# Attention and retention on 64 rows: the products of two heads issued alternately

## The chip, the cores and the metric

The kernel runs on one core of a Trainium2 chip. The metric is the device time of one execution, in microseconds; of several runs the median is given. One further execution was recorded by the hardware profiler; its span is the time from its first to its last instruction. The engines are named as in the profile: PE is the tensor engine (PEld its loading of the stationary operand), DVE the vector engine, ACT the scalar engine, POOL the third compute engine, SP the one that issues transfers.

## The reference, cut to what matters

The kernel computes one inference step of a two-layer diffusion backbone on 256 latent and 128 context tokens with 1024 features, in float32. Layer 0 projects the normed tokens to two groups of eight heads of 64 features each. Group A is attention, group B retention, a linear attention with a decay by distance:

```
s_loc = einsum('bhrjqd,bhrwjkd->bhrjqwk', qg, band(k)) * scale + bias     # latent queries: a window of latents
s_ctx = einsum('bhrjqd,bhpd->bhrjqp', qg, k_ctx) * scale                  # ... and all context keys
p = softmax(concatenate([s_loc, s_ctx]))                                  # context queries: context keys alone
o_A = p @ v

att = einsum('bhid,bhjd->bhij', q, k) * dmask                             # group B, per direction
o_B = att @ v + (q * q_dec) @ s                                           # s: the cached state
o_B = rmsnorm(o_forward + o_backward) * silu(g)
y = concatenate([o_A, o_B]) @ w_out
```

Each sub-layer stands between two RMS norms and is followed by a SwiGLU channel mixer; layer 1 is a gated linear recurrence. Both are as before in the change.

## The kernel before, in words

Activations lie feature-major: 128 features of a tile in the partitions, 384 tokens along them. A tile of queries or keys thus holds two heads: the even one in partitions 0 to 63, the odd one in 64 to 127. Products with weights are split into three (`wh*hh`, `wh*hl`, `wl*hh`) in float32r; the products of attention and retention are plain float32, and each shows as two records in the trace.

The program is written as streams (generators) that yield instructions. A list scheduler (`Machine`, lines 102 to 199) merges them into one order per engine: it keeps a rough clock of each engine and takes next the stream whose head could start first; `margin` says how long before its turn a product's operands must be ready. A tuple that a stream yields is emitted in one piece. `products()` (line 1428) is the stream of the weight products: the in-projection in parts (`va` and `vb` token-major, with the tokens stationary, then the rest), gates, output projection. Weights are split into a high and a low part by ACT (`wh`, line 237) and DVE or, while a norm is under way, POOL (`wl`, lines 245 and 243). In free places DVE forms the modulation of later sub-layers by dot products (`mod_dve`, line 604, tile `mscr`), PE forms another part of it (`mod_pe`, tile `mraw`).

- `attention(h)`, line 952, one stream per head: three products into two of the eight PSUM banks (latent queries 0 to 127 with the 384 keys, the context queries with the context keys, latent queries 128 to 255), then bias, maximum, exponential and scaling on DVE and ACT, and seven transposes (`cb,as`, line 223). There are two score buffers `as`, so two heads can be under way. `attended(hp)`, line 1000, multiplies the values of two heads; its outputs have 64 rows, and the two heads are issued alternately already (`pt,va`, `pt,vc`).
- `retention(hp)`, line 1018, one stream per pair of heads, two sets of buffers. Lines 1055 to 1074 take the heads one after the other: decay matrix on DVE and ACT, two products of 256 columns into one bank (line 1066), their multiplication by the decay (`ro`, `at`), a product of 128 columns into another bank (line 1071), its multiplication (`kd`). The products with the values close the pair.
- `retention_norm`, line 1085: sums of squares of all heads on PE, root on ACT, reciprocal on DVE, spread back by PE (`scr,cse`), then per tile two multiplications and the split into `hh` and `hl`, for which the output projection waits.

The next norm and the channel mixer's first products follow (`Norm`, `ffn_products`).

Of the kernel before, what the change touches and what calls it, by code (L numbers as in the profile page):

```python
"""Two-layer hybrid diffusion backbone (neighbourhood attention + retention, then HGRN2) on one core.

Activations are kept feature-major: [128 features of a tile, tile, 384 tokens], the 256 latent
tokens first and the 128 context tokens after them. Products with the weights run as float32r:
each operand is split exactly into a high and a low part (w = wh + wl, x = xh + xl) and
wh*xh + wh*xl + wl*xh is accumulated.

The program is written as streams of instructions (generators). A list scheduler merges them into
one order per engine: it keeps a rough clock per engine and per region of memory, and of the next
instructions of all streams it takes the one that could start first. Tile adds the waits.  # L10

Each sub-layer starts its first group of products on x * g * (1 + scale), before the norm of x is
known; the reciprocal norm multiplies those products when they leave PSUM, and the shift comes in
as two more columns of the moving operand (one per condition). Later products use the normed h.
"""
# [18 lines left out]
P = 128  # L34
D = 1024
KT = 8            # feature tiles of D
NS = 256          # latent tokens
NP = 128          # context tokens
NT = NS + NP
NX = NT + 2       # and a column for the shift of either condition  # L40
FT = 22           # feature tiles of D_FF
# [6 lines left out]
# ------------------------------------------------------------------ the list scheduler  # L48
def region(ap):
    """name of the memory, first and last partition, first and last element"""  # L50
# [12 lines left out]
class Op:  # L63
    """one instruction: engine, call, what it writes and reads, time it holds the engine"""
# [8 lines left out]
# the order of emission: when loads may start, how long before its turn a stream's product must be ready  # L73
# [15 lines left out]
# from the end of an instruction to the start of one that waits for it, by engine: leaving, arriving  # L89
LEAVE = {"PE": 0.2, "DVE": 0.13, "ACT": 0.14, "POOL": 0.08, "SP": 0.9}  # L90
ARRIVE = {"PE": 0.15, "DVE": 0.0, "ACT": 0.0, "POOL": 0.05, "SP": 0.0}
# the tensor engine runs at half its clock at first
# [9 lines left out]
class Machine:  # L102
# [53 lines left out]
    def advance(self, s):  # L156
        """make the next instructions of a stream known; False if it waits, None if it is over"""
# [51 lines left out]
class Build:  # L209
    """instructions, not yet emitted"""  # L210
# [4 lines left out]
    def mm(self, out, lhsT, rhs, start=True, stop=True):  # L215
        n = width(rhs)
        cost = n * (1 if rhs.dtype == F32R and n >= 256 else 4) / 2400
        cost *= {32: 0.3, 64: 0.56}.get(out.shape[0], 1.0)
# [69 lines left out]
# ------------------------------------------------------------------ plans of weight chunks  # L288
def plan_kouter(ms, nk, n=4):
    """groups of n output tiles, k outside"""  # L290
    flat = [(k, m) for g in range(0, len(ms), n) for k in range(nk) for m in ms[g:g + n]]
    return [flat[i:i + 8] for i in range(0, len(flat), 8)]


def plan_kinner(ms, nk):
    """one output tile after the other"""
# [4 lines left out]
# even in-projection: 28 tiles: qa 0-3 ka 4-7 va 8-11 qb 12-15 kb 16-19 vb 20-23 gb 24-27  # L301
PLAN_E1 = plan_kouter([4, 5, 6, 7, 0, 1], KT, 6)
PLAN_E2 = plan_kouter([8, 9, 10, 11], KT)          # va, token-major
PLAN_E3 = plan_kinner([2, 3], KT)
PLAN_E4 = plan_kinner([12, 16, 13, 17, 14, 18, 15, 19], KT)
PLAN_E5 = plan_kouter([20, 21, 22, 23], KT)        # vb, token-major
PLAN_E6 = plan_kinner([24, 25, 26, 27], KT)
PLAN_EVEN = [PLAN_E1, PLAN_E2, PLAN_E5, PLAN_E3, PLAN_E4, PLAN_E6]
# odd in-projection: 40 tiles: q 0-7 ff 8-15 fb 16-23 i 24-31 g 32-39
PLAN_O1 = plan_kouter([0, 8, 16, 1, 9, 17], KT, 6)  # L310
PLAN_O2 = [plan_kouter(list(range(24 + 4 * g, 28 + 4 * g)), KT) for g in range(2)]      # i, token-major
# [159 lines left out]
def emit_all(nc, tc, ctx, io, outs):  # L471
# [480 lines left out]
    def attention(h):  # L952
# [42 lines left out]
        if h % 2 == 1:  # L995
            M.spawn(attended(hp), 3, margin=M_ATT)
# [596 lines left out]
```

## Time and profile before

| | us |
|---|---|
| runs, median of 3 (lowest, highest) | 1171.53 (1168.97, 1172.67) |
| span of the profiled execution | 1170.4 |
| PE busy | 1102.9 |
| DVE busy | 862.5 |
| ACT busy | 535.5 |
| POOL busy | 211.9 |

The profile gives no other time of its execution than the span, which lies inside the range of the runs. "Busy" is the union of an engine's instructions; matmuls are pipelined and the ends of their records are modelled, so the distance from the start of one product to the start of the next says more than a record's length. All float32 products of attention and retention have the line of the helper that records them, L219; they are told apart by the tiles: `bank<-ka,qa` are attention's scores, `bank<-qk` retention's.

### The profile page before, as it was taken

Reading aid. Unit: us, or ns where it says so; the run is one execution under the profiler, and the core shown is the slowest. Engines: PE = TensorE matmul, PEld = TensorE weight load, DVE = VectorE, ACT = ScalarE, POOL = GpSimd, SP = SyncE. Lnnn points to the kernel's source line nnn. Section 1 sums busy time; section 2 is a strip of 40 time slices with the busy share of each in tenths; the row PEclk is TensorE's granted clock in tenths of the full one; section 3 lists DMA queues with packets and bytes.
Section 4 is the critical chain, followed back from the end, with each engine's and each line's share of the span. In section 5 each row is a group of like instructions: output and inputs, shape, how many; then the busy total and the mean of one; then the engine's idle time right before and its main releaser. Section 6 shows DMA issues by size and latency. Waiting matters only on the chain. (4 is left out here: it accounts for less than half of the span.)

```text
span 1170.4 us, 18358 instructions
## 1 busy us (share of the span) xinstructions
PE 1102.9 (94%) x7012; PEld 1018.2 (87%) x7012; DVE 862.5 (74%) x1615; ACT 535.5 (46%) x1010; POOL 211.9 (18%) x192
## 2 busy tenths in 40 slices
PE   7999999998799999999959999999997999999996
PEld 5768887887799999998947988889987999999995
DVE  2698887678999999884898589997778644443343
ACT  3675544445433333334654555665555433333231
POOL 1210000036200000000655134352027200000001
PEclk9999999989899999999989999999999999999998
DMA  8965545343377677674231332222222343334331
GB/s 338 367 210 204 178 159 179 119 163 115 122 259 241 238 237 247 228 264 171 99 99 55 104 100 83 86 82 95 96 91 90 110 131 119 129 123 135 129 115 54
DMA packets 49688, 180.43 MB, mean 154 GB/s; under 512 B 6561, under 2 KB 13729, under 8 KB 43073
## 3 DMA queue, kind: packets, MB, share of 16 engines
q1 hardware_dynamic: 49536, 179.18, 44.9%
q8 instruction: 55, 0.90, 0.3%
q14 instruction: 33, 0.26, 0.1%
q0 software_dynamic: 64, 0.08, 0.0%
HBM read 174.79 MB, written 3.41 MB: 152 GB/s over the span
## 5 line engine op out<-in xcount | busy, mean ns | idle before, releaser
L219 PE MATMUL bank<-hh,wh 128*128 128x384 f32 (+1 forms) x1248 | 441.0, 353 | 11.4 <-DVE wb L262 8.5
L219 PE MATMUL bank<-hl,wh 128*128 128x384 f32 (+1 forms) x1248 | 427.6, 343 | 6.0 <-DVE hl L245 6.0
L219 PE MATMUL bank<-hh,wl 128*128 128x384 f32 (+1 forms) x1248 | 426.0, 341 | 0.7 <-POOL wl L243 0.7
L245 DVE TENSOR_TENSOR wl<-wr,wh 128x1024 fp32r<-128x1024 f32 x190 | 233.8, 1231 | 121.9 <-ACT wh L237 121.9
L237 ACT ACTIVATE wh<-wr 128x1024 fp32r<-128x1024 f32 x216 | 227.7, 1054 | 157.1 <-PE bank L219 116.2
L219 PEld LDWEIGHTS bank<-hh,wh 128*128 128x128 f32 x1248 | 238.8, 191 | 26.9 <-DVE wb L262 9.1
L219 PEld LDWEIGHTS bank<-hl,wh 128*128 128x128 f32 x1248 | 239.3, 192 | 8.5 <-DVE hl L245 8.1
L219 PEld LDWEIGHTS bank<-hh,wl 128*128 128x128 f32 x1248 | 239.7, 192 | 1.1 <-POOL wl L243 1.1
L258 DVE SCALAR_TENSOR_TENSOR mscr<-mraw,msb 128x1024 f32<-128x1024 f32 x128 | 157.9, 1233 | 2.3 <-ACT msb L237 1.2
L243 POOL TENSOR_TENSOR wl<-wr,wh 128x1024 fp32r<-128x1024 f32 x26 | 64.3, 2476 | 513.0 <-ACT wh L237 507.6
L219 PE MATMUL bank<-gh,wl 128*128 128x384 f32 x352 | 117.6, 334 | 0.0
L219 PE MATMUL bank<-gl,wh 128*128 128x384 f32 x352 | 117.6, 334 | 0.0
L219 PE MATMUL bank<-gh,wh 128*128 128x384 f32 x352 | 117.6, 334 | 0.0
L219 PEld LDWEIGHTS bank<-gh,wh 128*128 128x128 f32 x352 | 66.1, 188 | 0.0
L219 PEld LDWEIGHTS bank<-gl,wh 128*128 128x128 f32 x352 | 66.1, 188 | 0.0
L219 PEld LDWEIGHTS bank<-gh,wl 128*128 128x128 f32 x352 | 66.1, 188 | 0.0
L237 ACT ACTIVATE fs<-bank 128x384 f32<-128x384 f32 x38 | 18.7, 492 | 89.1 <-PE bank L219 89.1
L237 ACT ACTIVATE gh<-fs 128x384 fp32r<-128x384 f32 x44 | 22.9, 519 | 72.3 <-DVE fs L245 58.3
L237 ACT ACTIVATE scr<-bank 128x384 f32<-128x384 f32 x44 | 21.7, 492 | 61.6 <-PE bank L219 60.8
L219 PE MATMUL bank<-wh,hl 128*128 128x512 f32 x96 | 40.4, 421 | 9.2 <-DVE hl L245 9.1
L243 POOL TENSOR_TENSOR x<-x,fy 128x384 f32<-128x384 f32 x4 | 4.5, 1150 | 242.6 <-DVE fy L245 242.6
L245 DVE TENSOR_TENSOR fs<-bank,fs 128x384 f32<-128x384 f32 x38 | 21.2, 558 | 36.2 <-PE bank L219 35.0
(222 smaller groups left out, 1432.8 us busy)
## 6 DMA issues: line engine op xcount, KB each, us to landing
mraw<-in_w_mod SPq DMA_DIRECT2D x48, 1024.0 KB, 5.9
wr<-in_w_ffn_in SPq DMA_DIRECT2D x88, 512.0 KB, 3.3
wr<-in_w_ffn_out SPq DMA_DIRECT2D x44, 512.0 KB, 3.4
wr<-in_w_in_odd SPq DMA_DIRECT2D x40, 512.0 KB, 3.3
wr<-in_w_in_even SPq DMA_DIRECT2D x28, 512.0 KB, 5.3
wr<-in_w_out_even SPq DMA_DIRECT2D x8, 512.0 KB, 3.3
wr<-in_w_out_odd SPq DMA_DIRECT2D x8, 512.0 KB, 3.3
bias<-in_bias SPq DMA_DIRECT2D x8, 384.0 KB, 4.0
```

Source lines behind the costliest of these rows:

```text
L219: return Op("PE", lambda: self.nc.tensor.matmul(out, lhsT=lhsT, rhs=rhs, start=start, stop=stop), [out], [lhsT, rhs], cost + 0.004)
L237: return Op("ACT", lambda: self.nc.scalar.activation(out, in_, func, **kw), outs, ins, 0.1 + width(in_) / 1200, table)
L243: return Op("POOL", lambda: self.nc.gpsimd.tensor_tensor(out=out, in0=a, in1=b, op=op), [out], [a, b], 0.12 + n * 0.0021)
L245: return Op("DVE", lambda: self.nc.vector.tensor_tensor(out=out, in0=a, in1=b, op=op), [out], [a, b], 0.06 + n / 960)
L258: return Op("DVE", lambda: self.nc.vector.scalar_tensor_tensor(out=out, in0=a, scalar=s, in1=b, op0=op0, op1=op1, **kw), outs, ins, 0.1 + ...
```

## The change

Attention's stream is per pair of heads: it takes two score buffers and four banks and issues the three products of both heads alternately, the even head from partitions 0 to 63, the odd one from 64 to 127, into different banks; what follows per head is a stream of its own, `probabilities`. Retention takes two decay buffers and two banks, forms both decay matrices first, issues its products alternately, and puts the 128-column products into the same two banks as the 256-column ones. The scheduler's cost of a product with 64 rows is set as that of one with 64 columns. Comments are removed throughout.

```diff
-        cost *= {32: 0.3, 64: 0.56}.get(out.shape[0], 1.0)
+        cost *= {32: 0.3, 64: 0.56}.get(min(out.shape[0], lhsT.shape[0]), 1.0)
...
-    def attention(h):
-        hp, j = h // 2, h % 2
-        a, b = 64 * j, 64 * j + 64
+    def attention(hp):
         qa, ka = L0.qa, L0.ka
-        res, = yield from L0.heads.take()
+        yield lambda: "ctx" in ev and ("qa", hp) in ev and ("ka", hp) in ev
+        res = yield from L0.heads.take(2)
+        bs = yield from banks.take(4)
+        for out, q, k in ((lambda j: bs[2 * j][:, :NT], (0, P), (0, NT)), (lambda j: bs[2 * j + 1][:, :NT], (P, NS), (0, NT)),
+                          (lambda j: bs[2 * j][:, NT:512], (NS, NT), (NT, 512))):
+            yield tuple(I.mm(out(j), qa[64 * j:64 * j + 64, hp, q[0]:q[1]], ka[64 * j:64 * j + 64, hp, k[0]:k[1]]) for j in range(2))
+        for j in range(2):
+            M.spawn(probabilities(2 * hp + j, res[j], bs[2 * j], bs[2 * j + 1]), P_ATT + 0.01 * (2 * hp + j), margin=M_ATT)
+    def probabilities(h, res, b0, b1):
         s, mx, sm = res
-        yield lambda: "ctx" in ev and ("qa", hp) in ev and ("ka", hp) in ev and len(L0.biases) > 0
-        bias = L0.biases.popleft()
-        b0, b1 = yield from banks.take(2)
-        yield (I.mm(b0[:, :NT], qa[a:b, hp, 0:P], ka[a:b, hp, :NT]),)
-        yield (I.mm(b0[:, NT:512], qa[a:b, hp, NS:NT], ka[a:b, hp, NT:512]),)
-        yield (I.mm(b1[:, :NT], qa[a:b, hp, P:NS], ka[a:b, hp, :NT]),)
+        yield lambda: len(L0.biases) > 0 and L0.biases[0][0] == h
+        bias = L0.biases.popleft()[1]
...
-        for j in range(2):
+        rows = [slice(64 * j, 64 * j + 64) for j in range(2)]
+        dts = yield from scr.take(2)
+        for j, dt in enumerate(dts):
             h = 2 * hp + j
-            a, e = 64 * j, 64 * j + 64
-            dt, = yield from scr.take()
             yield I.ts(dt, cse[:, E_DP:E_DP + NT], L0.rdb[:, 0, h:h + 1], MUL)
...
-            b, = yield from banks.take()
-            for n, s_ in ((0, 1), (1, 0)):
-                yield I.mm(b[:, NS * n:NS * n + NS], k[a:e, P * s_:P * s_ + P], q[a:e, :NS])
+        bs = yield from banks.take(2)
+        yield tuple(I.mm(bs[j][:, NS * n:NS * n + NS], k[rows[j], P * s_:P * s_ + P], q[rows[j], :NS])
+                    for n, s_ in ((0, 1), (1, 0)) for j in range(2))
+        for j in range(2):
             for n in range(2):
-                yield I.tt(ats[j][:, n], b[:, NS * n:NS * n + NS], dt[:, P * n:P * n + NS], MUL)
-            banks.give(b)
-            b, = yield from banks.take()
-            yield I.mm(b[:, :P], k[a:e, NS:NT], q[a:e, NS:NT])
-            yield I.tt(ap_[:, j], b[:, :P], dt[:, P:2 * P], MUL)
-            banks.give(b)
-            scr.give(dt)
+                yield I.tt(ats[j][:, n], bs[j][:, NS * n:NS * n + NS], dts[j][:, P * n:P * n + NS], MUL)
+        yield tuple(I.mm(bs[j][:, :P], k[rows[j], NS:NT], q[rows[j], NS:NT]) for j in range(2))
+        for j in range(2):
+            yield I.tt(ap_[:, j], bs[j][:, :P], dts[j][:, P:2 * P], MUL)
+        banks.give(*bs)
+        scr.give(*dts)
...
-        for h in range(8):
-            M.spawn(attention(h), P_ATT + 0.01 * h, margin=M_ATT)
+        for hp in range(4):
+            M.spawn(attention(hp), P_ATT + 0.02 * hp, margin=M_ATT)
```

The scheduler makes a new order of it, from the first attention products to the middle of layer 1. On PE, the end of a value group (`pt`) and the scores of one head that follow it stood so before:

```order
L219 MATMUL bank_63<-pt_147,vc 64x256
L219 MATMUL bank_63<-pt_146,va 64x128
L219 MATMUL bank_63<-pt_147,va 64x128
L219 MATMUL bank_68<-ka,qa 128x384
L219 MATMUL bank_68<-ka,qa 128x128
L219 MATMUL bank_66<-ka,qa 128x384
L219 MATMUL bank_70<-wh_108,hh 128x512
```

and so now, for the second pair:

```order
L219 MATMUL bank_67<-pt_147,vc 64x256
L219 MATMUL bank_67<-pt_146,va 64x128
L219 MATMUL bank_67<-pt_147,va 64x128
L219 MATMUL bank_65<-ka,qa 128x384
L219 MATMUL bank_66<-ka,qa 128x384
L219 MATMUL bank_69<-ka,qa 128x128
L219 MATMUL bank_64<-ka,qa 128x128
L219 MATMUL bank_68<-wh_109,hh 128x512
```

These are the last four products of the pair; its first two, into banks 69 and 64, stand ahead of the value group. The third and the fourth pair stand in the same way, the first pair in one piece. Behind the second pair's last products 15 token-major and 24 feature-major weight products follow before its first transposes.

In retention on PE, a head's two groups before:

```order
L219 MATMUL bank_70<-qk 128x256 x2
L219 MATMUL bank_65<-hh,wh_108 128x384
L219 MATMUL bank_65<-hl,wh_108 128x384
L219 MATMUL bank_65<-hh,wl_111 128x384
L219 MATMUL bank_69<-qk 128x128
```

and a pair's now:

```order
L219 MATMUL bank_64<-qk 128x256
L219 MATMUL bank_63<-qk 128x256
L219 MATMUL bank_64<-qk 128x256
L219 MATMUL bank_63<-qk 128x256
L219 MATMUL bank_67<-hh,wh_110 128x384
L219 MATMUL bank_67<-hl,wh_110 128x384
L219 MATMUL bank_67<-hh,wl_113 128x384
L219 MATMUL bank_65<-qd_156,s_153 128x256 x2
L219 MATMUL bank_64<-qk 128x128
L219 MATMUL bank_63<-qk 128x128
```

Four products now stand between two weight products where two stood, and the 128-column ones return to the banks of the others. Between a pair's two groups the order has 6, 6, 3 and 12 weight products.

On DVE, from the last retention step (`kd`) to the operand of the retention norm's product (`scr<-rs,cb`), before:

```order
L245 TENSOR_TENSOR kd_154<-bank_65,scr_92 128x128
L245 TENSOR_TENSOR wl_111<-wr_105,wh_108 128x1024
L268 RECIPROCAL rs_86<-rs_86 128x96
L245 TENSOR_TENSOR scr_91<-rs_86,cb 128x384
L245 TENSOR_TENSOR wl_112<-wr_106,wh_109 128x1024
```

and now:

```order
L245 TENSOR_TENSOR kd_154<-bank_67,scr_88 128x128
L245 TENSOR_TENSOR mod_80<-macc_131,bmod 128x2x2
L258 SCALAR_TENSOR_TENSOR mod_80<-mod_80,gn 128x2
L258 SCALAR_TENSOR_TENSOR mscr_130,macc_132<-mraw_103,msb_129 128x1024 x3
L245 TENSOR_TENSOR wl_111<-wr_105,wh_108 128x1024
L268 RECIPROCAL rs_86<-rs_86 128x96
L258 SCALAR_TENSOR_TENSOR mscr_130,macc_132<-mraw_103,msb_129 128x1024
L245 TENSOR_TENSOR wl_112<-wr_106,wh_109 128x1024
L245 TENSOR_TENSOR scr_91<-rs_86,cb 128x384
```

Four dot products of the first phase moved here from earlier places, and a weight split passed the norm's operand. Further on, at the start of the channel mixer, the second pair of modulation chunks that PE forms (`mraw`) moved behind the first 15 weight products, and 54 weight products instead of 87 stand on PE ahead of the second norm's last step. In layer 1 the order of the mixers' products differs in places; the counts of all instructions on PE, ACT and SP are the same, and two weight splits moved from POOL to DVE.

## Rows read from the trace of the kernel before

**Rows 1.** From the page: busy time, share of the span and instructions of each engine.

```profile
PE 1102.9 (94%) x7012; PEld 1018.2 (87%) x7012; DVE 862.5 (74%) x1615; ACT 535.5 (46%) x1010; POOL 211.9 (18%) x192
```

**Rows 2.** Busy time by stretch: from and to (us from the span's start), length, busy time of PE, PEld, DVE, ACT and POOL (instructions), granted clock of PE, share and GB/s of DMA.

```profile
74.60:130.00 55.40, 55.08 (x300) 42.97 (x298) 51.27 (x108) 34.66 (x72) 0.00 (x0) 1.00 0.64 210
130.00:195.00 65.00, 65.00 (x393) 54.00 (x393) 54.99 (x116) 28.75 (x55) 0.00 (x0) 1.00 0.50 165
195.00:212.00 17.00, 17.00 (x106) 13.99 (x105) 9.96 (x19) 10.72 (x16) 0.00 (x0) 1.00 0.38 147
...
226.00:249.40 23.40, 22.10 (x165) 20.21 (x163) 16.94 (x32) 9.60 (x17) 2.36 (x1) 1.00 0.50 164
249.40:256.30 6.90, 6.47 (x19) 6.07 (x20) 6.90 (x18) 4.34 (x15) 2.98 (x3) 0.51 0.50 209
```

**Rows 3.** PE's longest wait from 67 to 226 us: total, times, longest.

```profile
PE bank L219 <- ACT qa L237: 1.1, 1, 1.1
```

**Rows 4.** The modulation's dot products on DVE (instructions that write mscr) in the stretches 74.6 to 130, 130 to 195 and 195 to 212 us: sum of their lengths, sum and mean of DVE's busy time.

```profile
sum 137.40, DVE 39.31; mean DVE 13.10
```

**Rows 5.** PE in order of time around a head that stands alone (`ka,qa`), its first transposes (`cb,as`), and a value group (`pt`) with the next head behind it: start, us, operation, shapes, count of records.

```profile
82.39 0.39 PE L219 MATMUL bank<-wl,hh 128*128 128x512 f32 x1
82.63 0.39 PE L219 MATMUL bank<-wh,hl 128*128 128x512 f32 x1
82.94 1.78 PE L219 MATMUL bank<-ka,qa 64*128 64x384 f32 x6
84.65 0.50 PE L219 MATMUL bank<-wh,hh 128*128 128x512 f32 x1
84.99 0.39 PE L219 MATMUL bank<-wl,hh 128*128 128x512 f32 x1
...
87.55 0.60 PE L223 MATMUL bank<-cb,as 128*128 128x128 f32 x4
...
89.80 1.08 PE L219 MATMUL bank<-pt,va 128*64 128x256 f32 x8
...
91.47 1.78 PE L219 MATMUL bank<-ka,qa 64*128 64x384 f32 x6
```

**Rows 6.** The same around two heads that are queued one behind the other.

```profile
110.21 2.53 PE L219 MATMUL bank<-ka,qa 64*128 64x384 f32 x12
112.68 0.45 PE L219 MATMUL bank<-hh,wh 128*128 128x384 f32 x1
```

**Rows 7.** The same around heads 0 and 1.

```profile
66.98 0.92 PE L219 MATMUL bank<-ka,qa 64*128 64x384 f32 x4
69.04 1.15 PE L219 MATMUL bank<-ka,qa 64*128 64x128 f32 x8 [1.14 <-ACT qa L237]
70.12 0.50 PE L219 MATMUL bank<-wh,hh 128*128 128x512 f32 x1
```

**Rows 8.** The same around the two groups of one retention head (`qk`).

```profile
151.75 1.13 PE L219 MATMUL bank<-qk 64*128 64x256 f32 x4
152.81 0.44 PE L219 MATMUL bank<-hh,wh 128*128 128x384 f32 x1
...
154.06 0.48 PE L219 MATMUL bank<-qk 64*128 64x128 f32 x2
154.48 0.44 PE L219 MATMUL bank<-hh,wh 128*128 128x384 f32 x1
```

**Rows 9.** The same, where the records of two retention heads share a burst.

```profile
163.10 1.13 PE L219 MATMUL bank<-qk 64*128 64x128 f32 x6
```

**Rows 10.** DVE in order of time: one dot product.

```profile
79.84 1.22 DVE L258 SCALAR_TENSOR_TENSOR mscr<-mraw,msb 128x1024 f32<-128x1024 f32 x1
```

**Rows 11.** DVE in order of time around the retention norm.

```profile
203.23 0.76 DVE L245 TENSOR_TENSOR at<-bank,scr 128x256 f32<-128x256 f32 x2 [1.22 <-PE bank L219]
204.37 0.29 DVE L245 TENSOR_TENSOR kd<-bank,scr 128x128 f32<-128x128 f32 x1 [0.38 <-PE bank L219]
207.67 1.23 DVE L245 TENSOR_TENSOR wl<-wr,wh 128x1024 fp32r<-128x1024 f32 x1 [3.01 <-ACT wh L237]
...
210.11 0.56 DVE L245 TENSOR_TENSOR scr<-rs,cb 128x384 f32<-128x384 f32 x1
```

**Rows 12.** ACT in order of time: the root of the retention norm.

```profile
208.95 0.34 ACT L237 ACTIVATE rs<-bank,eps 128x96 f32<-128x96 f32 x1
```

**Rows 13.** PE in order of time at the first product of the retention norm.

```profile
212.25 0.34 PE L219 MATMUL bank<-hh,wl 128*128 128x384 f32 x1
212.42 0.81 PE L219 MATMUL bank<-scr,cse 128*128 128x384 f32 x2
```

**Rows 14.** PE's two longest waits from 249 to 311 us, the start of the first channel mixer.

```profile
PE bank L219 <- DVE hl L245: 5.2, 2, 5.0
PE bank L219 <- DVE wb L262: 3.2, 1, 3.2
```

**Rows 15.** Busy time in the stretch from a norm's first sums to steady products, in the first and in the second channel mixer (columns as in rows 2).

```profile
243.50:310.90 67.40, 54.11 (x312) 50.01 (x312) 61.33 (x103) 35.93 (x74) 37.99 (x23) 0.85 0.36 126
...
861.00:919.10 58.10, 48.31 (x290) 44.92 (x282) 52.22 (x91) 33.94 (x72) 35.47 (x22) 0.91 0.21 68
```

**Rows 16.** DVE on the scores `as` of all eight heads: count, ns min/median/max, first and last start, shapes.

```profile
L251 DVE TENSOR_SCALAR as<-as,sm x24: 279/414/423, 74.7 to 143.4; 128x384 f32<-128x384 f32 x16, 128x128 f32<-128x128 f32 x8
L245 DVE TENSOR_TENSOR as<-bank,bias x16: 529/552/558, 69.9 to 131.7; 128x384 f32<-128x384 f32 x16
```

More of the change, by code (lines that the diff above doesn't have):

```diff
@@ L457 @@
 class Bag:
+    pass
 HALVES = ((1, 0, NS), (0, NS, NT))
@@ L912, in load_bias @@
             yield I.dma(b, io["bias"][h])
-            L0.biases.append(b)
+            L0.biases.append((h, b))
     L0.biases = deque()
@@ L994, in attention @@
         L0.ptof[h] = pt
-        if h % 2 == 1:
-            M.spawn(attended(hp), 3, margin=M_ATT)
+        if 2 * (h // 2) in L0.ptof and 2 * (h // 2) + 1 in L0.ptof:
+            M.spawn(attended(h // 2), 3, margin=M_ATT)
     L0.ptof = {}
```

## The prediction

> **What bounds the kernel now.** I read the page first: over the whole span PE is busy 94%, DVE 74% [rows 1]. An average says little here, so next I read the table of busy time by stretch, to see who is full where the change acts. The attention products run from 67 to 130 us and the retention products from 152 to 204 us. From 74.6 to 212 us PE is busy 137.08 of 137.40 us at a granted clock of 1.00, the upper level of 2.4 GHz [rows 2], and its longest wait from 67 to 226 us is 1.1 us, for a query tile [rows 3]. So in this stage the tensor engine alone sets the pace: a microsecond taken off PE moves everything behind it, as long as the other engines can follow. DVE is the nearest: 116.2 of the same 137.4 us. But 39.31 us of that are dot products of the modulation (mscr) [rows 4], which the scheduler puts where DVE is free; without them DVE is needed for 77 us.
>
> **What one product with 64 rows costs now.** Then I read PE's own order of time around the products that change. A lone head of attention (three products) starts 1.71 us before the next weight product (82.94 to 84.65), and four of the eight heads stand so [rows 5]. Two heads queued one behind the other, without alternation, take 2.47 us (110.21 to 112.68), not 3.42 [rows 6]: the halves of the array already overlap where the queue reaches the second head in time. And in one place the old order happens to alternate: heads 0 and 1 share their first four records in one burst of 0.92 us, and, after the wait for the query, the other eight in 1.15 us [rows 7]; together 2.07 us for two heads, where a lone head's burst lasts 1.78. Alternation on this chip is thus seen, not hoped for: a second head costs almost nothing.
>
> Retention: one head's two 256-column products take 1.06 us (151.75 to 152.81) and its 128-column product 0.42 us (154.06 to 154.48) [rows 8]. In one place, 163.10, two heads' records fell into one burst, 1.13 us long, and one 128-column product went free [rows 9].
>
> **Part 1, attention.** Before: 3.14 us for heads 0 and 1 (66.98 to 70.12, the wait included), 4 x 1.71 and 2.47: 12.4 us. After: the first pair runs its two pairs of 384 columns while it waits for the query, and of what follows the wait only a 128-column pair is left, which I price as the retention group of that size, 0.42: it ends at 69.46 instead of 70.12, 0.66 us less. In the other three pairs the order shows the first two products ahead of another pair's value products and the last four behind them, so a pair is two bursts: 2.07 less the two tails of 0.07 that the next product covers, 1.93 us. Three of them, 5.8, replace 9.3. **Attention: -4.2 us.** Bounds for a pair: 1.71 (one burst, a free second head) and 2.47 (no gain over queued heads); I take 1.93 because it is measured on alternating products.
>
> **Part 2, retention.** Before 8 x 1.06 + 7 x 0.42 = 11.4 us. After: four pairs at the price of one head, 4 x 1.48 = 5.9. **-5.5 us.** The bad end takes the ratio of the queued heads, 2.47/1.71, for each pair: 8.5, which leaves -2.9.
>
> **Part 3, changes of shape.** Around each such group PE loses time beyond it: the last weight product before it holds the engine 0.31 us (82.63 to 82.94) where the one ahead of that took 0.24, the first one after it 0.34 (84.65 to 84.99) [rows 5], 0.17 us together. Retention goes from 15 groups to 8: 7 x 0.17 = 1.2. In attention three lone groups and one lone value group vanish (-0.7), while four more boundaries between scores and values appear, at the 0.1 of such an edge (+0.4). **-1.5 us.**
>
> **Part 4, what the change adds.** In the order of DVE after the last retention pair, three dot products and a weight split now stand before the reciprocal of the retention norm, and one of each between it and the next step. A dot product takes 1.22 us, a split 1.23 [rows 10, 11]. Before, DVE's last retention step ended at 204.66 and the root was ready at 209.29 [rows 11, 12], a gap of 4.63; the three (3.7), the split (1.2) and two small steps (0.3) overrun it by 0.6 us, and the next two add 2.45. The norm's product on PE began at 212.42, 1.75 us after its operand (210.67) [rows 11, 13], so this much is slack: 3.05 - 1.75 = **+1.3 us**, since behind the 24 weight products that the order puts here PE has only the products that wait for this chain. Below: 0, if DVE gets through these while it would wait; above: 3.05, if the slack is gone.
>
> The 128-column products of retention now go into the banks of the 256-column ones, and so wait until DVE has multiplied those out: four multiplications, in rows of two at 0.76 us [rows 11], 1.5 us, under six weight products (1.05 us) and the change of shape. The order puts three to twelve weight products there. **+0.4 us** in all; below 0, above 4 x 1.0.
>
> Costed at nothing: the taking of two score buffers and four banks at once (its cover is the weight products that the order puts behind each pair; see the third rival), the new cost of a 64-row product in the scheduler's table (it only moves the order), the bias tables now named by head.
>
> **Sum:** -4.2 - 5.5 - 1.5 + 1.3 + 0.4 = -9.5 us on the profiled execution, whose span of 1170.4 becomes 1160.9. The median of the runs shown, 1171.53, lies 1.1 us above that span; I keep the 1.1: **1162.0 us**.
>
> **Rivals.**
> 1. *The channel mixer's start gives more, or takes some back.* Behind the stage PE stalls on the norm: 8.4 us of waits for DVE alone between 249 and 311 us [rows 14]. The same code takes 67.4 us at its first use and 58.1 at its second [rows 15], so 9.3 us hang on order alone here. The new order has the second modulation pair behind the first 15 weight products, and the second norm's root after 54 of them instead of 87. Gain taken at half of the 9.3, with the rest as forecast: 1157. Loss of the same size: 1167.
> 2. *DVE becomes the bound.* It must now do the same in some 10 us less: 116.2 of 127. Against it stand the 39 us that can move; for it, that the scheduler puts them where it believes DVE idle, and each holds DVE 1.22 us without a break [rows 10]. If one of them delays every one of the eight heads' chains in part, half of the gain goes: 1167. The Trainium skill has this as a rule: its page TensorEngine Tiling (Array Packing), section PSUM Bottleneck, says that tiling speeds up TensorE but not the evacuation of PSUM, which may then become the bottleneck. By that rule the time would be this rival's; no run so far shows the changed kernel, and the 77 us of needed DVE work in the trace speak against it.
> 3. *Slower: a pair of heads starves PE.* Now a pair holds both score buffers, so the next cannot start until both heads are transposed. One head's way from its products to its first transposes was 4.6 us (82.94 to 87.55) [rows 5]; the second adds on DVE at least its two additions at 0.55 and three scalings at 0.41, 0.41 and 0.28 [rows 16], 2.2 us: 6.8. Behind the second pair's products the order has about 10.4 us of PE work (a value group of 1.67 [rows 5], 1.08 of scores [rows 7], 15 products at 0.24 [rows 5] and 24 at 0.17 [rows 13]). Three dot products in that chain use up the margin of 3.6; with six, PE would idle 3.7 us in each of three pairs, and after 1.3 us idle in the 23.4 before 249.4 the granted clock stood near its lower level (1.2 GHz), at 0.51, for 6.9 us [rows 2], which costs half of that. 3 x (3.7 + 3.4) = 21 against 9.5: 1183. It decides from the fourth dot product on, in every pair; in the old order PE idled nowhere in attention after 74.6 us but for 0.3 us [rows 2].
> 4. *The pairs do not overlap.* Then a pair costs two heads: attention 4 x 3.42 = 13.7 (+1.3), retention 11.8 (+0.4), less 1.5, plus 1.7: 1173.4. [Rows 6, 7] speak plainly against it.
>
> **How the numbers follow.** Forecast with its bounds 0.61; more gain at the mixer's start 0.13; less there 0.08; DVE 0.11; starved PE 0.04; no overlap 0.03. The likeliest gives the time, 1162.0. The cases of the forecast alone span from -11.9 (one-burst pairs, part 4 at zero) to 0 (all bad ends at once); the range that leaves out 2 in 10 is **1155 to 1168.5**: below, the second case with a little more than its half; above, the two cases at 1167. A change of less than 0.3% (3.5 us) can't be told from none in this kernel. Faster by more (below 1168.0): nearly all of the forecast, the second case and most of the two at 1167: 0.82. Within it 0.12, slower 0.06.
>
> **What would show it.** In the profile after: bursts of 0.92 and 1.15 us for a pair in attention, 1.13 and 0.49 in retention, their PE time down from 23.8 to 13 or 14 us; no PE idle between 75 and 205; the first sums of the next norm, now at 243.5 [rows 15], 9 to 10 us earlier; DVE fuller, with dot products up to the retention norm. I am wrong if a pair's burst lasts over 2.4 us, if PE idles by several microseconds before 205, or if the gain is there at the first norm and gone when the channel mixer's products run steadily (from 311 us before).

## The result, and the profile after

The changed kernel takes 1165.45 us (median; 1164.34 to 1166.98), the kernel before 1171.46 beside it: a ratio of 0.9949 with a 95% interval of 0.9933 to 0.9964. Its profiled execution spans 1165.1 us where the one before spans 1170.4. So it is faster, by 6.0 us where 9.5 were forecast. The direction held, and so did the mechanism for the score products; the price of the 128-column products was too small, and idle PE and its clock, which the sum had at nothing, cost time.

The page's busy line hardly moves against [rows 1]. A share of 94% on PE says nothing of where 5 us went:

```profile
PE 1100.3 (94%) x7012; PEld 1018.7 (87%) x7012; DVE 865.2 (74%) x1617; ACT 534.5 (46%) x1010; POOL 206.7 (18%) x190
```

**Attention.** PE in order of time, the first pair of heads and the second (columns as in rows 5, in brackets the idle time ahead and its releaser):

```profile
66.70 1.56 PE L219 MATMUL bank<-ka,qa 64*128 64x384 f32 x8
68.77 0.49 PE L219 MATMUL bank<-ka,qa 64*128 64x128 f32 x4 [0.51 <-ACT qa L237]
69.19 0.50 PE L219 MATMUL bank<-wh,hh 128*128 128x512 f32 x1
...
90.36 0.92 PE L219 MATMUL bank<-ka,qa 64*128 64x384 f32 x4
91.20 1.08 PE L219 MATMUL bank<-pt,va 128*64 128x256 f32 x8
...
92.87 1.14 PE L219 MATMUL bank<-ka,qa 64*128 64x384 f32 x8
93.93 0.50 PE L219 MATMUL bank<-wh,hh 128*128 128x512 f32 x1
```

The 0.92 and 1.15 us of the prediction are there. From a burst's start to the next product it is 0.84 and 1.06 us for two heads, where a lone head took 1.71 [rows 5]. The seven bursts add up to 8.22 us; before it was 12.43 (the waits for the query, 0.51 and 1.14, included).

**Retention.** The first pair on PE, and DVE at the same moments:

```profile
147.68 1.13 PE L219 MATMUL bank<-qk 64*128 64x256 f32 x8
148.74 0.44 PE L219 MATMUL bank<-hh,wh 128*128 128x384 f32 x1
...
150.00 0.80 PE L219 MATMUL bank<-qk 64*128 64x128 f32 x4
```

```profile
148.84 0.76 DVE L245 TENSOR_TENSOR ro<-bank,scr 128x256 f32<-128x256 f32 x2 [1.13 <-PE bank L219]
149.51 0.75 DVE L245 TENSOR_TENSOR at<-bank,scr 128x256 f32<-128x256 f32 x2
```

The 256-column group of two heads takes what one head took, 1.06 us [rows 8]. The 128-column group does not: 0.80 instead of the forecast 0.49. Its single records start at 150.00 and 150.21 for one head and at 150.32 and 150.53 for the other, so they run one after the other. DVE leaves the first head's bank (`ro`) at 149.60 and the second one's (`at`) at 150.26, and the second product starts 0.06 us after that.

**Idle PE where the prediction wanted none.** PE's order of time at the third pair and in the retention norm, and DVE's ahead of the third pair:

```profile
181.53 1.13 PE L219 MATMUL bank<-qd,s 128*128 128x256 f32 x4 [0.90 <-DVE qd L245]
183.00 0.49 PE L219 MATMUL bank<-qk 64*128 64x128 f32 x2 [0.34 <-DVE ro L245]
183.66 0.48 PE L219 MATMUL bank<-qk 64*128 64x128 f32 x2 [0.18 <-DVE at L245]
...
208.31 0.44 PE L219 MATMUL bank<-hh,wh 128*128 128x384 f32 x1 [1.15 <-ACT hh L237]
```

```profile
178.51 1.22 DVE L258 SCALAR_TENSOR_TENSOR mscr<-mraw,msb 128x1024 f32<-128x1024 f32 x1
...
180.79 0.68 DVE L245 TENSOR_TENSOR qd<-qd,qk 128x512 f32<-128x512 f32 x1
181.39 1.22 DVE L245 TENSOR_TENSOR wl<-wr,wh 128x1024 fp32r<-128x1024 f32 x1
182.53 0.42 DVE L245 TENSOR_TENSOR ro<-bank,scr 128x256 f32<-128x256 f32 x1
```

A dot product stands in front of `qd`, and a weight split between `qd` and the multiplication that frees the bank. By stretch (columns as in rows 2), the clock falls behind it to its lower level, 1.2 GHz, for 3.42 us (below: half clock):

```profile
74.60:130.50 55.90, 55.90 (x332) 46.77 (x332) 49.94 (x103) 35.26 (x77) 0.00 (x0) 1.00 0.61 211
130.50:195.30 64.80, 63.39 (x394) 53.69 (x390) 55.01 (x118) 30.71 (x63) 0.00 (x0) 0.97 0.40 132
...
184.36:187.78 3.42, 3.42 (x17) 2.53 (x14) 2.32 (x6) 1.26 (x3) 0.00 (x0) 0.50 0.23 92
```

In the retention norm PE waits for something other than the prediction's chain on DVE. The operand of the norm's product (`scr<-rs,cb`) is ready at 204.97, before PE comes to that product at 205.60; the 1.15 us lie behind the product, on the way over DVE and ACT to `hh` (the three engines in order of time):

```profile
204.42 0.55 DVE L245 TENSOR_TENSOR scr<-rs,cb 128x384 f32<-128x384 f32 x1
205.60 1.56 PE L219 MATMUL bank<-scr,cse 128*128 128x384 f32 x4
206.55 0.56 DVE L245 TENSOR_TENSOR qk<-qk,bank 128x384 f32<-128x384 f32 x1 [1.32 <-PE bank L219]
207.74 0.52 ACT L237 ACTIVATE hh<-qk 128x384 fp32r<-128x384 f32 x1 [2.15 <-DVE qk L245]
```

Before, three weight products and a group of modulation products (212.78 to 214.69) stood there and covered this way:

```profile
213.69 1.07 PE L219 MATMUL bank<-mraw,sc 128*32 128x256 f32 x16
```

**The channel mixer's start.** From the norm's first sums to the 300th weight product behind them, of after and then of before:

```profile
235.90:319.80 83.90, 70.49 (x414) 65.48 (x414) 74.45 (x132) 42.72 (x84) 35.03 (x21) 0.86 0.43 154
```

```profile
243.50:324.40 80.90, 67.61 (x390) 63.51 (x390) 72.62 (x122) 41.77 (x83) 37.99 (x23) 0.87 0.40 134
```

It holds 24 more records and takes 3.0 us longer. PE's longest waits there, to be read against [rows 14], have other names now; the wait for `mod` is for the second modulation pair, 2.44 us at 254.13:

```profile
PE bank L219 <- DVE wb L262: 7.2, 2, 6.3
PE bank L219 <- DVE mod L245: 2.8, 2, 2.4
PE bank L219 <- ACT hh L237: 1.3, 1, 1.3
```

**The sum, from the records.** I walked over all PE records from the first score product to the next norm's first sums, gave each the time to the start of the next one, and set apart idle time and half of the busy time in every half-clock stretch. The same for the kernels of runs e5 to e7 below:

| us | before | after | e5 | e6 | e7 |
|---|---|---|---|---|---|
| lead to the first score product | 66.98 | 66.70 | 66.89 | 66.44 | 66.86 |
| attention scores | 11.28 | 7.72 | 7.72 | 7.72 | 7.72 |
| retention scores | 11.37 | 7.48 | 6.37 | 7.47 | 6.37 |
| 627 weight products | 124.73 | 122.84 | 122.92 | 122.15 | 122.28 |
| modulation pair on PE | 2.95 | 1.00 | 1.00 | 2.81 | 2.81 |
| retention norm's products | 2.72 | 3.47 | 3.47 | 4.04 | 4.04 |
| all other products | 21.97 | 21.72 | 22.21 | 21.73 | 22.20 |
| idle | 1.46 | 3.22 | 2.65 | 2.86 | 2.67 |
| lost to half clock | 0 | 1.71 | 0 | 1.71 | 0 |
| first sums at | 243.46 | 235.86 | 233.23 | 236.93 | 234.95 |

Behind them, to the next layer's first sums: before 304.86 us, after 307.82, e6 303.71. Of the 2.96 us that after loses here, modulation products that used to stand ahead of the sums take 1.88 (5.08 against 3.20), half clock 1.48 (9.32 against 7.84), idle time 0.12 (13.41 against 13.29); the other products give 0.53 back. In e12, the same kernel once more, the stretch takes 307.43 us, with 5.25 of modulation, 5.66 of half clock and 16.04 idle: between two executions of one kernel idle time and half clock trade places, the moved products stay. In e6 the modulation costs 3.20, half clock 6.09 and idle time 13.64. The rest of the span changes by -0.83 us in layer 1, +0.59 in its channel mixer and -0.4 at the end.

### The profile page after: what moved, and what is told of

Same layout as the page of the kernel before. It is cut to its first block, busy times and chain, and to the rows that moved or that the text cites. A ratio compares the mean times of both kernels' runs of the same rounds, so it can differ in the third digit from the quotient of the medians.

```text
span 1165.1 us, 18376 instructions
## 1 busy us (share of the span) xinstructions
PE 1100.3 (94%) x7012; PEld 1018.7 (87%) x7012; DVE 865.2 (74%) x1617; ACT 534.5 (46%) x1010; POOL 206.7 (18%) x190
## 4 chain that ended last, share of the span: by engine, by line
PE 78%; DVE 13%; issue 3%; DMA 2%; ACT 2%; POOL 1%; SPq 1%; DVEq 0%; POOLq 0%; ACTq 0%
PE bank L219 77%; DVE scr L251 2%; DVE hl L245 2%; DVE x L245 2%; DVE hl L258 2%; DMA bias<-in_bias 1%; PE bank L223 1%; DMA mraw<-in_w_mod 1%; DVE fy L245 1%; POOL wl L243 1%; DMA wr<-in_w_in_even 1%; SPq L284 1%; DVE XB L245 0%; DVE wl L245 0%; DVE mscr L258 0%
## 5 line engine op out<-in xcount | busy, mean ns | idle before, releaser
L245 DVE TENSOR_TENSOR wl<-wr,wh 128x1024 fp32r<-128x1024 f32 x192 | 236.2, 1231 | 121.1 <-ACT wh L237 121.1
L219 PEld LDWEIGHTS bank<-hh,wh 128*128 128x128 f32 x1248 | 240.3, 193 | 32.9 <-DVE wb L262 13.6
L243 POOL TENSOR_TENSOR wl<-wr,wh 128x1024 fp32r<-128x1024 f32 x24 | 60.0, 2503 | 511.3 <-ACT wh L237 505.4
L237 ACT ACTIVATE gh<-fs 128x384 fp32r<-128x384 f32 x44 | 22.7, 518 | 65.7 <-DVE fs L245 57.5
L251 DVE TENSOR_SCALAR scr<-scr,mod 128x256 f32<-128x256 f32 (+1 forms) x64 | 41.7, 696 | 10.9 <-POOL scr L243 10.6
```

What stands on the lines that cost most here:

```text
L219: return Op("PE", lambda: self.nc.tensor.matmul(out, lhsT=lhsT, rhs=rhs, start=start, stop=stop), [out], [lhsT, rhs], cost + 0.004)
L237: return Op("ACT", lambda: self.nc.scalar.activation(out, in_, func, **kw), outs, ins, 0.1 + width(in_) / 1200, table)
L243: return Op("POOL", lambda: self.nc.gpsimd.tensor_tensor(out=out, in0=a, in1=b, op=op), [out], [a, b], 0.12 + n * 0.0021)
L245: return Op("DVE", lambda: self.nc.vector.tensor_tensor(out=out, in0=a, in1=b, op=op), [out], [a, b], 0.06 + n / 960)
L251: return Op("DVE", lambda: self.nc.vector.tensor_scalar(out=out, in0=a, scalar1=s1, scalar2=s2, op0=op0, **kw), [out], ins, 0.19 + width(o ...
```

## Experiments

All ratios are to the kernel before, run on the same chip beside each. Where "order kept" is said, every engine's order is that of the kernel compared with, written out as a list, so that nothing else moves.

**e1, e2: each half alone.** e1 keeps the new `attention` and puts the old `retention` back; e2 the other way round, both with the new price.

> Attention in pairs, retention as before. Theory (the gain hangs on where the list scheduler puts the last retention pair): the order has that pair and its norm chain behind the last of the 672 in-projection products, where PE has nothing else, so some 7 of the 10.35 us from the last score products to the norm's products (195.26 to 205.61 in the changed kernel) show as idle PE; attention's -4.2 and -0.3 for shapes against +7: about 1173 us. Rival (the parts add up): 1167, and PE idles nowhere near 200 us.

> Retention in pairs, attention as before, with the new price of a 64-row product. The order again has the last retention pair behind all in-projection products. Theory as for the run above: retention's -3.7 and -1.2 for shapes against +7 of idle PE: about 1173 us. Rival (the parts add up): 1166.5.

e1: 1170.85 us, 1.0000 (0.9992 to 1.0009), between the theory's 1173 and the rival's 1167. e2: 1179.72, 1.0082 (1.0070 to 1.0094), far over both. The parts do not add up. In e1 attention's gain is there in full (7.72 us) and is given back behind the last retention pair, on PE:

```profile
208.93 0.37 PE L219 MATMUL bank<-scr,cse 128*32 128x96 f32 x8 [1.17 <-ACT scr L237]
...
211.97 1.62 PE L219 MATMUL bank<-scr,cse 128*128 128x384 f32 x2 [1.80 <-DVE scr L245]
```

and by the clock right after:

```profile
212.03:218.85 6.82, 6.82 (x19) 4.90 (x20) 3.06 (x8) 1.05 (x2) 0.00 (x0) 0.50 0.58 207
```

In e2 the waits at that place (2.5, 2.0 and 1.2 us) stand with 20.5 us at the lower level, which I had left out; the 2.0 lies ahead of them, the other two inside. The lower level costs half of the 15.80 us in which PE is busy there, 7.9 us:

```profile
209.68:230.16 20.48, 15.80 (x56) 10.98 (x57) 6.90 (x16) 3.69 (x7) 0.00 (x0) 0.50 0.33 135
```

So my 7 us of idle PE were 3.0 in e1, with 3.4 lost to the clock behind them; in e2 the 7 were there, the clock's 7.9 came on top, and another 3.7 us of idle PE lie between 140 and 187 us. That the place of the last pair costs this is read from the traces; no run moved that pair alone.

**e8: the new price alone**, `min(out.shape[0], lhsT.shape[0])` in the kernel before.

> The kernel before with nothing but the new price of a 64-row product in the scheduler's table. My prediction put it at nothing. Its order has the last retention pair and the norm's chain behind the last in-projection product, as in the run with retention alone. Theory (where that pair stands decides): several microseconds of idle PE and a half clock at 200 to 230 us: 1176 to 1182 us. Rival (the price only moves the order, the sum of work is the same): 1170 to 1173.

1172.53 us, 1.0018 (1.0007 to 1.0029): 2.1 us slower. The wait that I foresaw is there (1.7 us for `at`, then a half clock from 209.52 for 3.4 us), but in size the rival was right. "Costed at nothing" is thus nearly right, and by no means a promise.

**e3: the order inside a pair.**

```diff
-  h0 a, h1 a, h0 b, h1 b     (each pair's first four products)
+  h0 a, h0 b, h1 a, h1 b     (the order of everything else as in the changed kernel)
```

> The changed kernel with the order of everything kept, except that the two heads' products of a pair stand one head behind the other and no longer alternate. Theory (alternation is what lets the halves overlap; heads queued one behind the other overlap in part, 2.47 us for two by the kernel before): each of the 4 attention bursts and each of the 4 retention bursts of 1.06 us grows by 0.4 to 0.5 us: 1168.5 to 1169.5 us. Rival (any two neighbours from different halves overlap, the order inside a pair is of no account): within 0.6 us of the changed kernel, 1165 to 1166.

1167.33 us, 0.9968 (0.9956 to 0.9980), 2.2 us above the changed kernel by ratios, between theory and rival; the two intervals overlap, but from the first score product to the first sums it is 171.09 us against 169.16 (168.99 in e12). The two stages answer differently. PE at the second attention pair and at the first retention pair:

```profile
89.52 1.55 PE L219 MATMUL bank<-ka,qa 64*128 64x384 f32 x4
91.01 1.08 PE L219 MATMUL bank<-pt,va 128*64 128x256 f32 x8
...
92.67 1.78 PE L219 MATMUL bank<-ka,qa 64*128 64x384 f32 x8
...
150.68 1.14 PE L219 MATMUL bank<-qk 64*128 64x256 f32 x8
```

In retention, head by head, the eight records still take 1.14 us: with two products of each head the order inside the pair is of no account, as the rival said. In attention the value products lie between the two bursts, so the edit parted the heads, and only the 128-column products still overlap: 3.19 us a pair instead of 1.91, 3.84 in all attention. The first pair, whose first eight records stand in one burst, took 2.48 us (2.49 when alternated). So what counts is that the other half's products follow with nothing of another shape between, and how soon. The kernel before shows the second: at 110.21 [rows 6] three products of one head stand ahead of the other's. The second head's first record starts 0.76 us after the first one's, when three of the first head's six records are still to come, and the two heads take 2.46 us instead of 1.71. That case e3 did not repeat, so the theory's 2.47 is not refuted for it. The whole run loses less than 3.84 since it has no half clock near 184 us (idle there 0.55, 0.34 and 0.17 us).

**e4: DVE relieved.** The dot products of the first phase run over 256 of 1024 columns.

> The changed kernel with the order of everything kept; the 32 dot products of the first phase of the modulation run over 256 of their 1024 columns, so three quarters of that sum are left out. DVE gets some 29 us back between 75 and 205 us. Theory (what is missing from the retention gain is DVE arriving late: the dot products stand before what PE waits for): the idle PE at 181 to 188 us, the waits of the 128-column products and the 1.15 us in the retention norm go, the first sums of the next norm come 4 to 5.5 us earlier than 235.86, and the second modulation pair's weights are loaded earlier: 1158 to 1161 us. Rival (PE alone sets the pace there): first sums within 1 us of 235.86, 1164 to 1166.

1162.77 us, 0.9940 (0.9925 to 0.9954). That lies between theory and rival. The dot products between 75 and 205 us fall from 39.2 to 13.6 us of DVE's time. Counted from the first score product, the first sums come 2.15 us earlier: 1.71 of it the half clock, which is gone, 0.5 from the wait for `qd`. The other waits stand as they were:

```profile
PE bank L219 <- ACT hh L237: 1.1, 1, 1.1
PE bank L219 <- DVE qd L245: 0.4, 1, 0.4
PE bank L219 <- DVE ro L245: 0.3, 1, 0.3
PE bank L219 <- DVE at L245: 0.2, 1, 0.2
```

My theory of late dot products falls for all but that one place: the 128-column bursts are still 0.80 us, the norm still waits 1.15, and the second modulation pair is as late as before.

**e5: other banks for the 128-column products** of the first three pairs, order kept.

```diff
+        if len(banks.q) > 1:
+            banks.give(*bs)
+            bs = [banks.q.popleft() for j in range(2)]
         yield tuple(I.mm(bs[j][:, :P], k[rows[j], NS:NT], q[rows[j], NS:NT]) for j in range(2))
```

> The changed kernel with the order of everything kept; for the first three pairs of heads the 128-column retention products go into two free banks instead of those of the 256-column products (for the fourth pair only one bank is free, so it stays). Theory (the second head's product waits until DVE has read its bank, so the two run one after the other): the bursts of 0.73, 0.74 and 1.08 us become 0.42 to 0.45, the fourth stays at 0.84; with the idle 0.34 and 0.18 at 183 us gone, 1.2 us less at the next norm's first sums (235.86 to 234.7), and about 1.7 us more if the half clock at 184 to 188 us goes too: 1163 to 1164.5 us. Rival (the two products can't overlap at that size, or wait for something other than the bank): bursts as before, 1165 to 1166.

1163.51 us, 0.9938 (0.9925 to 0.9950). The burst is what the forecast said:

```profile
150.17 0.49 PE L247 MATMUL bank<-qk 64*128 64x128 f32 x4
```

Three bursts fell from 0.73, 0.74 and 1.08 us to 0.42; the fourth, left in its banks, stays at 0.85. The 0.34 and 0.18 us of idle time at 183 us are gone, and so is the half clock. Shown, then: the wait is for the bank. From the first score product to the first sums it is 2.82 us less: 1.71 of half clock, 1.11 in the bursts and 0.57 of idle time, but the value products behind the third pair take 0.49 more. They now wait for DVE themselves: the first `at` is written at 182.80 and its product starts at 182.85. In the total the 1.3 us against the changed kernel lie inside the two intervals, so it is the trace that shows the gain.

The fourth pair waits for its bank too, although 12 weight products stand between its groups: in the changed kernel a weight split of 1.22 us stands on DVE between the two heads' multiplications, the second bank comes free at 195.00, and the product starts at 195.05.

**e6: the first modulation pair early** (the scheduler's delay of it left out).

```diff
     def mod_late():
-        if mods.n < 8:
+        if mods.n < 10:
             return 0.0
```

> The changed kernel with one number of the scheduler changed: the first modulation pair on PE is no longer put off by 0.6 us, so its second chunk stands in the retention norm instead of behind the next norm's first sums, as in the kernel before. Everything ahead of it stays. Theory (the gain is lost in the channel mixer's start because the second pair comes late): the 300th weight product after the first sums comes 80.9 us after them instead of 83.91, the idle 2.44 at 254 us and 6.26 at 289 us are replaced by the waits of the kernel before, and the chunk covers 0.5 to 1 of the 1.15 us idle at 208 us: 1161 to 1162.5 us. Rival (the start is bound by DVE's and POOL's own work, the pair's place is of no account): 1165 to 1166.

1160.39 us, 0.9910 (0.9897 to 0.9924), 4.6 us less than the changed kernel by ratios. The mixer's start has its old shape and 79.80 us:

```profile
236.90:316.70 79.80, 66.16 (x389) 62.16 (x389) 71.63 (x122) 41.88 (x83) 37.89 (x23) 0.89 0.41 142
```

Counted from the first score product, the first sums come 1.33 us later than in the changed kernel, since the pair's products stand ahead of them again; the 1.15 us of idle time in the retention norm was not covered. From there to the next layer it is 4.11 us less: net 2.8 us, about the 3 of the theory. Another 2.75 came in layer 1 (308.27 us instead of 311.02; 310.17 in e12), where the edit also changed the order: 1.6 of it half clock, 0.4 idle time, 0.8 weight products. That part was not expected, and what in the new order brings it was not tested.

**e7: both.**

> Both edits of the two runs above, in the order of the second. Theory: they add up, -1.2 to -2.9 and -3 to -4.5 against the changed kernel: 1159.5 to 1161 us. Rival (what one gives is idle time that the other takes up): no better than the better of the two.

1158.62 us, 0.9894 (0.9878 to 0.9909). -1.3 and -4.6 us against the changed kernel had been measured apart, -6.4 together: they add up within the intervals, and the time lies a little below the forecast.

**e9, e10, e11, e12: what is left in e7.** e9 puts a pair's six score products into one burst, e10 moves one dot product behind `qd`, e11 does both; e12 is the changed kernel once more.

> The kernel with both edits (own banks, early modulation), everything else in its order; the six score products of a pair of heads now stand in one burst ahead of the value products, where three of the four pairs had two bursts (0.85 and 1.07 us) around them. Theory (a burst costs its own tail and one change of shape): three pairs give 0.2 us each in the burst (1.71 instead of 1.92) and 0.1 to 0.17 at the edge: 1.0 us less, 1157.5. Rival (the value products then wait for what the scores covered, or the edge costs nothing): within 0.4 us of that kernel, 1158.2 to 1159.

> The kernel with both edits; one dot product of the modulation on DVE (1.2 us, at 178 us) stands seven operations later, behind the product with the decay (qd) for which PE then idles 0.88 us at 181 us. Theory (PE waits there for DVE alone, and behind it PE is full): 0.6 to 0.9 us less at the next norm's first sums (234.95): 1157.8. Rival (something else is late there, the wait moves): no change at the first sums.

> Both edits of the two runs above together. Theory: they add up to 1.6 to 1.9 us: 1156.8. Rival: the better of the two alone.

> The changed kernel once more, beside the three above on the same chip, so that differences of a microsecond are read against it: ratio to the kernel before 0.994 to 0.996.

1157.54 us, 0.9889 (0.9875 to 0.9902); 1157.23, 0.9888 (0.9875 to 0.9902); 1158.32, 0.9893 (0.9878 to 0.9908); and 1165.17, 0.9954 (0.9941 to 0.9966). The profiles are plainer than these times: in e9

```profile
89.52 1.78 PE L247 MATMUL bank<-ka,qa 64*128 64x384 f32 x12
91.23 0.65 PE L247 MATMUL bank<-pt,va 128*64 128x256 f32 x3
```

three pairs take 1.71 us instead of 1.91, 0.6 of the forecast 1.0. The weight products take 122.28 us in both; that tests no edge, since they have as many neighbours of another shape in e9 as in e7. The 0.2 us a pair is itself the cost of a burst's two ends: its first 384-column records are followed after 0.43 us instead of 0.32, and its last ones keep the engine some 0.1 longer than those in the middle. In e10 the wait for `qd` falls from 0.88 to 0.44. From the first score product to the first sums it is 168.09 us in e7, 167.50 in e9, 167.59 in e10 (0.5 less, where 0.6 to 0.9 was forecast) and 167.03 in e11: there the two add up. In the total e9, e10, e11 and e7 can't be told apart. All four beat both kernels, the changed one by 0.5% to 0.7%.

## Why the prediction was right, and where its sizes were off

- **What bounds it: right.** PE's time in the two stages came off the span up to the first sums (-7.6 us of the forecast -9.5, but 1.95 of it are modulation products that only moved behind the sums), and PE is full from 74.6 to 130.5 us.
- **Part 1, attention: right to the tenth.** -4.2 forecast, 12.43 to 8.22 measured; -0.6 of it in the first pair, as priced.
- **Part 2, retention: the pair at the price of one head holds** for the 256-column products (1.06 us) and, as e5 shows, for the 128-column ones (0.42), but only in banks of their own.
- **Part 4, the same banks: this step failed in size.** I set four multiplications of DVE (1.5 us) against six weight products and priced the rest at 0.1 a pair. What I did not see is that the second head's bank comes free 0.66 us after the first one's, so the pair runs one after the other. In e5 three pairs gave 1.11 us in the bursts and 0.57 idle time; with the fourth (0.85 against 0.42) that is 2.1 us where 0.4 stood, and the half clock of 1.71 went with it. Not all of the 2.1 can be had: 0.49 came back in e5 in the value products.
- **Part 3, shapes: -1.5 forecast.** The 627 weight products take 1.89 us less. The records tell how much of it is edges: 110 of them stood next to a product of another shape, now 94, and beyond the median of those that don't (0.175 us for 384 columns, 0.23 for 512) they take 8.54 us before and 6.98 after, 1.6 less. The term held.
- **Part 4, the norm: +1.3 forecast, right by luck.** Idle 1.15 and 0.15 us, though not by the dot products that I blamed: the chain on DVE is done 0.63 us before PE needs it, and with dot products of a quarter of the length (e4) the wait is still 1.15. PE waits behind the norm's product, where the new order has nothing to cover the way to `hh`; this is read from the two orders, no run put work there.
- **No idle PE between 75 and 205: wrong** by 0.90, 0.34 and 0.18 us, and by the clock behind it.
- **Rival 1, the mixer takes some back: it came in addition**, 3.0 us of the 4.7 that I gave it. I had read the second pair's place in the order, and held it for a chance of 0.08. e6 shows that this place is the cause. In the sum it acts first through products moved (1.88), which the gain ahead of the sums had been credited with; idle time and half clock together add 1.6, in e12 0.6. My 9.3 us that "hang on order alone" were a misreading: the two stretches hold 312 and 290 PE records [rows 15], and over the whole way to the next norm's first sums the two mixers of the kernel before differ by 7.5 us (304.86 and 297.37).
- **Rival 2, DVE: in a few places, by its order.** DVE's reading decides when a bank may be written again (0.3 us in each of the first two pairs), a dot product delays `qd`, and a weight split the fourth pair's bank; e4 shows that the amount of dot products binds nothing but the wait for `qd` and the half clock behind it. The Trainium skill's rule (TensorEngine Tiling (Array Packing), section PSUM Bottleneck) is that the evacuation of PSUM may bind once tiling has sped up TensorE. In this trace that is a latency, not a lack of throughput.
- **Rival 3, starved PE: not seen** in attention. **Rival 4, no overlap: refuted** by the bursts.

In sum, by the table: -3.6 and -3.9 from the score products, -1.9 from the weight products around them, +1.8 idle, +1.7 half clock, -1.7 from everything else ahead of the sums (-1.95 of it modulation products that moved behind them, which came back as +1.88); that is the -7.6. Then +3.0 and -0.7: the span's -5.3, and -6.0 in the medians.

## What to carry to other kernels

Two products with 64 rows from the two halves of the partitions cost one here where they follow each other closely, with nothing of another shape between, into different banks. Behind two products of one head the other's still ran beside them; behind three it came 0.76 us late, so alternating is the safe order. A bank that another engine must empty first turns "side by side" into "one after the other". Where a scheduler writes the order, look up what else the new order moved, above all products and loads that used to fill a gap elsewhere, and price every new idle moment with the clock that may follow it. A half of a change, or its price table alone, can be slower than no change: here attention alone gave nothing, retention alone cost 0.8%, and both together gained.

## What was not expected of the hardware

- Two heads' products of 256 columns, queued head by head (four records, then four), take 1.14 us, and 1.13 when alternated: the second head's first record starts 13 ns after the first one's, not after its four. The Trainium skill says that different tiles can load weights and multiply in parallel (TensorEngine Tiling (Array Packing), section Tiling Modes); the trace agrees, and adds that with two products a head the order in the queue does not matter here. With three ahead it does: 0.76 us to the second head's first record in the kernel before.
- The stretch of half clock at 184 us (1.71 us lost) came behind idle times of 0.90, 0.34 and 0.18 us, in e12 behind 0.78, 0.34 and 0.17, in e6 behind 0.56, 0.34 and 0.17; in e3, behind 0.55, 0.34 and 0.17, it did not, nor in e4 behind 0.38, 0.34 and 0.18, nor behind a single 0.88 in e5 and e7. What decides between the nearly equal cases stays open.
- PE reaches the upper level of its clock at 14.9 to 17.5 us after the span's start (in the changed kernel at 17.1: weight products start 0.32 us apart before it and 0.18 behind it). With that the first score product lies between 65.7 and 67.0 us, although PE's order is the same up to there in all the kernels. Stages are therefore better compared from a mark inside the program than from the span's start.
